# SSM output reloaded into q's slots on SyncE's queue, and rotation tables staged in three tiles with own stores

## The chip, the cores and the metric

The kernel runs on one core of a Trainium2 chip. A core has five engines with their own instruction streams: TensorE (PE, matmuls), VectorE (DVE), ScalarE (ACT), GpSimd (POOL) and SyncE (SP). SP, ACT and POOL also issue DMA transfers, each on its own queue. The metric is the device time of one execution in microseconds (us), given as the median of several runs.

## The reference

One encoder layer over 512 tokens of width 1024, in float32: a half-step SwiGLU FFN, a mixer with two parallel branches (grouped-query attention and a bidirectional S5 state-space model, SSM), a second half-step FFN, and a gated per-layer embedding.

```python
h = h + 0.5 * swiglu(rms_norm(h, ffn1_norm[i]), ffn1_w_gate[i], ffn1_w_up[i], ffn1_w_down[i])
u = rms_norm(h, mix_norm[i])
proj = u @ w_in[i]
q, k, v, x_ssm, g_attn, g_ssm = jnp.split(proj, IN_SPLITS, axis=-1)
...
y_attn = block_gqa_attention(q, k, v).astype(x.dtype) @ w_attn_branch[i]
...
y_s5 = (y_fwd + y_bwd).reshape(b, s, SSM_WIDTH) + ssm_d[i].astype(f32) * x_ssm.astype(f32)
z = jax.nn.gelu(y_s5).astype(x.dtype)
z = z * jax.nn.sigmoid(z @ ssm_glu_w[i] + ssm_glu_b[i])
y_ssm = z @ w_ssm_branch[i]
merged = jax.nn.sigmoid(g_attn) * y_attn + jax.nn.sigmoid(g_ssm) * y_ssm
h = h + merged @ w_out[i]
h = h + 0.5 * swiglu(rms_norm(h, ffn2_norm[i]), ffn2_w_gate[i], ffn2_w_up[i], ffn2_w_down[i])
```

The SSM runs 32 groups of 16 channels with 64 complex states in both directions. The kernel turns it into matmuls over chunks of 8 tokens, for which it builds tables of powers of the complex step (rotation tables) out of the parameters.

## The kernel before

A float32 product is made as three matmuls: each operand is split into a high part (a cast by ACT, line 554, tiles ah, ph, xh, w_h, z) and the rest (a subtraction by DVE, line 555, al, pl, xl, w_l). So a matmul waits for ACT and then for DVE. The order of instructions on each engine is fixed when the kernel is built, by a scheduler that goes by the order of the program, priorities and its own costs. An engine works its own stream strictly in that order; a DMA queue of an issuing engine stands in the same stream, so an issue that has to wait holds what is behind it.

**First FFN (lines 697 to 745).** Tokens lie along the free axis, 512 wide. In each of two halves, eleven tiles f of 128 hidden features are made: gate product pg and up product pu (24 matmuls of 512 columns each), then DVE multiplies each by rb (lines 721 and 723), ACT takes silu (722), DVE multiplies (724), and ah and al are split off. Then come eight down products pd, each over all eleven ah and al.

**SSM parameters (ssm_params).** A generator whose steps are interleaved with the first FFN by `side`. For four sets gh of eight groups, DVE builds the powers T by doubling (lines 285 to 296; the next set begins with the memsets at line 277 and needs ACT's copies out of T to be over). Each set is then laid out as two tables b of 128 partitions by 1280 numbers in a tile tst (tag w3, two buffers): DVE writes a decay part (303 to 305), ACT copies six pieces out of T (307 to 309), and ACT's queue stores the tile of 640 KB to d_tb in device memory (310). POOL's queue in the same time moves other parameter tables (d_at, d_bt, d_a, d_b).

**Mixer.** The input projection w_in is made in pieces: the SSM's input (X), k and v, q, and sixteen gates of 128 features (proj_T, 24 matmuls pi each). DVE prepares trig and gq into tg (lines 860 to 863), and after the last norm sum ss the token scales rs (586 to 592), dg and, by a matmul pb, the row scale rb. The SSM's blocks give Z, which SP stores to zs_d (985). Attention runs by heads: `scores(hd)` makes products sc, exps p and row sums; their reciprocals go through device memory (r_d stored at 968 in pieces of 4 bytes, R loaded at 1018, both on POOL). `values(hd)` transposes p into ppt, splits ph and pl, and multiplies by vhl into po. While a head runs, one filler runs beside it (`fill`): four gates, then the GLU (`z_load`, `half` with w_ssm_glu), then the branch weights. `z_load` (1026) loads hb, the GLU's bias, and zT, four tiles of 256 KB of the SSM's output, into slots x4l to x7l, which hold the normed input for the gates until the last gate is done; then z is split off zT and the GLU's products pg run. Slots q0 to q7 hold qT of the eight heads.

Of the kernel before, what the change touches and what calls it, by code (L numbers as in the profile page):

```python
# [7 lines left out]
F32 = mybir.dt.float32  # L8
# [9 lines left out]
P = 128  # L18
SEQ = 512
G = 32  # L20
NS = 64
CH = 16
L = 8
NC_ = 64
GB = 4
NB = G // GB
TW = 5 * GB * NC_
# [18 lines left out]
def ssm_params(tc, nc, pk_, px, dp, k):  # L46
# [4 lines left out]
    d = {}  # L51
# [12 lines left out]
    pw = es.enter_context(tc.tile_pool(name="pw1", bufs=1, reuse_waits="tile"))  # L64
# [56 lines left out]
    n, q = expm1_parts(ls, s32, "d", -170.0, 170.0)  # L121
# [8 lines left out]
    n, q = expm1_parts(xr, s32, "x", -87.0, 88.0)  # L130
# [23 lines left out]
    f = math.factorial  # L154
# [103 lines left out]
    n, q = expm1_parts(xr, s32, "y", -87.0, 88.0)  # L258
# [16 lines left out]
    for gh in range(0, G, GH):  # L275
        T = pw.tile([P, 2, GH, NC_ + 2], F32, tag="T", name=f"T{gh}")
        V.memset(T[:, :, :, 0], 0.0)
        V.memset(T[:, :, :, NC_ + 1], 0.0)
        V.memset(T[:, 0, :, 1], 1.0)
        V.memset(T[:, 1, :, 1], 0.0)  # L280
        rkl = pw.tile([P, 2, GH], F32, tag="rkl", name=f"rkl{gh}")
        V.tensor_copy(rkl, rk[:, :, gh:gh + GH])
        n = 1
        tb = pw.tile([P, 2, 2, GH * NC_ // 2], F32, tag="tb", name=f"tbx{gh}")
        while n < NC_:
            br = rkl[:, 0].unsqueeze(2).broadcast_to([P, GH, n])
            bi = rkl[:, 1].unsqueeze(2).broadcast_to([P, GH, n])
            cmul2(T[:, 0, :, 1 + n:1 + 2 * n], T[:, 1, :, 1 + n:1 + 2 * n], T[:, :, :, 1:1 + n], br, bi,
                  tb[:, :, :, :GH * n].rearrange("p a r (g n) -> p a r g n", g=GH))
            n *= 2  # L290
            if n < NC_:
                sq = pw.tile([P, 2, GH], F32, tag="sq", bufs=2, name=f"sq{gh}_{n}")
                ta = pw.tile([P, 2, 2, GH], F32, tag="sqt", name=f"sqt{gh}_{n}")
                cmul2(sq[:, 0], sq[:, 1], rkl, rkl[:, 0], rkl[:, 1], ta)
                rkl = sq
            yield 1.0 + n / 20
        for b in range(gh // GB, (gh + GH) // GB):
            st = pw.tile([P, TW], F32, tag="w3", bufs=2, name=f"tst{b}")
            g0 = b * GB - gh
            N = GB * NC_  # L300
            v = lambda i, w=1: st[:, i * N:(i + w) * N].rearrange("p (g c) -> p g c", c=NC_)
            dv = v(4)
            V.tensor_copy(dv, e8[:, b * GB:(b + 1) * GB].unsqueeze(2).broadcast_to([P, GB, NC_]))
            V.memset(dv[:NS, :, 0], 0.0)
            V.memset(dv[NS:, :, NC_ - 1], 0.0)
            for ri in range(2):
                nc.scalar.copy(v(ri), T[:, ri, g0:g0 + GB, 1:NC_ + 1])
                nc.scalar.copy(v(2 + ri)[:NS], T[:NS, ri, g0:g0 + GB, 0:NC_])
                nc.scalar.copy(v(2 + ri)[NS:], T[NS:, ri, g0:g0 + GB, 2:NC_ + 2])
            nc.scalar.dma_start(d["tb"][b], st)  # L310
            yield 0.5
    es.close()
    pw = es.enter_context(tc.tile_pool(name="pw2", bufs=1, reuse_waits="tile"))
# [23 lines left out]
    for b in range(NB):  # L337
        gs = slice(b * GB, (b + 1) * GB)
# [11 lines left out]
        w3 = pw.tile([P, 3, GB, 2, P], BF16, tag="w3", bufs=2, name=f"wo3{b}")  # L350
# [21 lines left out]
    for m in range(G // 8):  # L372
        gs = slice(m * 8, (m + 1) * 8)
# [39 lines left out]
    for b in range(NB):  # L413
        gs = slice(b * GB, (b + 1) * GB)
# [8 lines left out]
        w3 = pw.tile([P, 3, GB, 2, P], BF16, tag="w3", bufs=2, name=f"wv3{b}")  # L423
# [94 lines left out]
def kernel(  # L518
# [6 lines left out]
    nc = tc.nc  # L525
    V, S, T = nc.vector, nc.scalar, nc.tensor
# [26 lines left out]
    def split(hi, lo, src):  # L553
        S.copy(hi, src)  # L554
        V.tensor_sub(lo, src, hi.bitcast(F32))  # L555
# [202 lines left out]
    with tc.tile_pool(name="f1", bufs=1, reuse_waits="tile") as fp, tc.tile_pool(name="pw", bufs=1, reuse_waits="tile") as pw:  # L758
# [18 lines left out]
        st = Stat()  # L777
# [17 lines left out]
    mp = mx.enter_context(tc.tile_pool(name="mp", bufs=1, reuse_waits="tile"))  # L795
    xs_d = dp.tile([SSMW, SEQ], F32, name="xs_d")
    zs_d = dp.tile([SSMW, SEQ], F32, name="zs_d")
    HH = HD // 2

    def slot(pool, tag, bufs, name, dt=F32):  # L800
        return pool.tile([P, SEQ], dt, tag=tag, bufs=bufs, name=uid(name))
# [11 lines left out]
    def run(*gens):  # L813

        gens = list(gens)
        while gens:
            gens = [g for g in gens if next(g, gens) is not gens]
# [13 lines left out]
    def gate(m):  # L831
# [5 lines left out]

        return proj_T(GA0 + m * P, done)

    ts = []  # L840
    ta = [cp.tile([P, SEQ], F32, tag=f"h{m}", name=f"ta{m}") for m in range(KT)]
    qT = [slot(mp, f"q{hd}", 1, "qT", F32R) for hd in range(NH)]
# [9 lines left out]
    with tc.tile_pool(name="qp", bufs=1, reuse_waits="tile") as qp:  # L852
# [39 lines left out]
        for q in range(4):  # L892
            gs = slice(q * G // 4, (q + 1) * G // 4)
# [52 lines left out]
    def scores(hd):  # L946

        g = hd // (NH // 2)
        pr = prs.setdefault(hd, [])
        nb = a0.tile([P, TT], F32, tag="nb", bufs=3, name=uid("nb"))  # L950
        if hd % 2 == 0:
            sums2[hd // 2] = a0.tile([P, 2, TT], F32, tag="s2", bufs=2, name=uid("s2"))
        sm = sums2[hd // 2][:, hd % 2]
        for t in range(TT):
            sc = bank("mm", uid("sc"))
            tk = slice(t * P, (t + 1) * P)
            T.matmul(sc, qT[hd][:, tk], kh[g], start=True, stop=False)
            T.matmul(sc, qT[hd][:, tk], kl[g], start=False, stop=True)  # L958
            V.tensor_reduce(nb[:, t:t + 1], sc, axis=AX.X, op=ALU.max, negate=True)  # L959
            V.tensor_mul(nb[:, t:t + 1], nb[:, t:t + 1], rq[:, t, hd:hd + 1])  # L960
            p_ = slot(pool_p[hd % 2], "pp", 4, "p")
            S.activation(p_, sc, AF.Exp, bias=nb[:, t:t + 1], scale=rq[:, t, hd:hd + 1], accum_out=sm[:, t:t + 1])  # L962
            pr.append(p_)
            yield
        if hd % 2 == 1:
            s2 = sums2[hd // 2]
            V.reciprocal(s2, s2)
            nc.gpsimd.dma_start(r_d[hd // 2].rearrange("h (t p) -> p h t", p=P), s2)
# [19 lines left out]
    at = mx.enter_context(tc.tile_pool(name="at", bufs=1, reuse_waits="tile"))  # L988
# [6 lines left out]
    def values(hd):  # L995
        pr = prs[hd]
        g = hd // (NH // 2)
        po = bank("pv", uid("po"))
        for kt in range(TT):
            pt = bank("pt", uid("ppt"))  # L1000
            for t in range(TT):
                T.transpose(pt[:, t * P:(t + 1) * P], pr[t][:, kt * P:(kt + 1) * P], ident)  # L1002
            ph, pl = ph_("ph", F32R), ph_("pl", F32R)
            split(ph, pl, pt)
            yield
            vv = vhl[:, kt, g].rearrange("p a d -> p (a d)")
            T.matmul(po, vv, ph, start=kt == 0, stop=False)  # L1007
            T.matmul(po, vv, pl, start=False, stop=kt == TT - 1)
        if hd % 2 == 0:
            po_of[hd // 2] = slot(at, "of", 3, "of")  # L1010
        of = po_of[hd // 2]
        ob = at.tile([HD, SEQ], F32, tag="ob", bufs=1, name=uid("ob"))
        S.copy(ob, po[HD:])
        V.tensor_add(of[(hd % 2) * HD:(hd % 2 + 1) * HD], po[:HD], ob)
        if hd % 2 == 1:
            R = at.tile([P, SEQ], F32, tag="R", bufs=1, name=uid("R"))
            for i in range(2):
                nc.gpsimd.dma_start(R[i * HD:(i + 1) * HD], r_d[hd // 2][i].partition_broadcast(HD))
            V.tensor_mul(of, of, R)
            ohl.append(tuple(slot(at, f"o{c}{hd // 2}", 1, "oT", F32R) for c in "hl"))  # L1020
            split(ohl[hd // 2][0], ohl[hd // 2][1], of)


    yhl, zs = [], []

    def z_load():
        xs_ = lambda k, c, name, dt=F32: slot(xp, f"x{k}{c}", 1, name, dt)
        hb = at.tile([P, 4], F32, name="hb")
        nc.gpsimd.dma_start(hb, w["ssm_glu_b"][0].rearrange("(m p) -> p m", p=P))
        V.tensor_scalar_mul(hb, hb, 0.5)  # L1030
        zs.append((hb, xs_))
        for m in range(4):
            zT = xs_(4 + m, "l", "zT")
            nc.gpsimd.dma_start(zT, zs_d[m * P:(m + 1) * P])
            zh, zl = xs_(m, "h", "z", F32R), xs_(m, "l", "z", F32R)
            split(zh, zl, zT)
            zs.append((zT, zh, zl))

    def half(ww, mc, x, done):

# [23 lines left out]
    def fill(i):  # L1064
        ng = 2 * KT - NG1 - NG2
        if i < ng:
            return gate(NG1 + NG2 + i)
        if i < ng + 2:
            if i == ng:
                z_load()  # L1070
            return half(w["ssm_glu_w"][0], i - ng, [z[1:] for z in zs[1:]], glu_done)
        if i < ng + 6:
            return half(w["w_ssm_branch"][0], i - ng - 2, yhl, ssm_done)
        return iter(())
# [15 lines left out]
        split(mg[m][0], mg[m][1], mt)  # L1090

    for hd in range(NH):
        run(values(hd), fill(hd), *([scores(hd + 1)] if hd < NH - 1 else []))
    for i in range(NH, 2 * KT - NG1 - NG2 + 6):
        run(fill(i))
# [2 lines left out]
    st = Stat()  # L1098
# [13 lines left out]
    with tc.tile_pool(name="f2", bufs=1, reuse_waits="tile") as fp:  # L1112
        st = Stat()
# [106 lines left out]
```

## Time and profile before

| | us |
|---|---|
| median of 3 runs | 1187.05 |
| lowest and highest run | 1185.81, 1188.17 |
| the profiled execution | 1185.39 |
| span of that execution, first to last instruction | 1183.6 |
| PE busy in the span | 1143.2 |
| DVE busy | 774.0 |
| ACT busy | 507.5 |
| POOL busy | 58.5 |

The profile tells what happened in one execution. Times of a timeline are us from the span's start. Busy time is the time in which an engine had an instruction at work; an idle time is given in front of the instruction that ended it, with the work whose end released it. A DMA's time runs from its issue to the landing of its last byte. PEclk is the clock that TensorE was granted, 1.0 being 2.4 GHz and 0.5 being 1.2 GHz; over a window it is a mean.

### The profile page before, as it was taken

How to read it: one execution, taken by the hardware profiler on the slowest of the kernel's cores; microseconds unless marked ns; L12 is line 12 of the kernel's file. 1: busy time of each engine (PE TensorE's matmuls, PEld its weight loads, DVE VectorE, ACT ScalarE, POOL GpSimd, SP SyncE). 2: the span in 40 equal slices, each digit the busy share in tenths (PEclk: the TensorE clock that was granted, in tenths of full speed). 3: DMA queues.
4: the chain of work that ended last, by engine and by line, in shares of the span. 5: the costliest groups of instructions: out<-in, count | busy, mean ns of one | idle time of the engine just before them, and what ended most of it. 6: DMA issues, size and time to landing. Idle time of an engine off the chain costs nothing.

```text
span 1183.6 us, 16482 instructions
## 1 busy us (share of the span) xinstructions
PE 1143.2 (97%) x6150; PEld 943.5 (80%) x6150; DVE 774.0 (65%) x1574; ACT 507.5 (43%) x919; POOL 58.5 (5%) x95
## 2 busy tenths in 40 slices
PE   8999989999999999978898999999999999999998
PEld 7888868888788888867676788888888888888886
DVE  4986798887589848989666867554443344444542
ACT  6484455444345437443656634342322223223331
POOL 1314100000000000000010000000000000000100
PEclk9999999999999999999997999999999999999999
DMA  8739865545968995887552245333323433323422
GB/s 190 171 92 313 256 221 178 161 142 107 271 228 268 298 193 157 250 251 224 132 86 62 45 105 164 88 98 91 89 74 99 128 100 96 88 64 98 157 57 54
DMA packets 253440, 175.97 MB, mean 149 GB/s; under 512 B 34896, under 2 KB 235792, under 8 KB 253360
## 3 DMA queue, kind: packets, MB, share of 16 engines
q1 hardware_dynamic: 246352, 153.20, 46.1%
q0 software_dynamic: 5392, 15.36, 5.0%
q10 hardware_dynamic: 1616, 6.36, 1.6%
q8 instruction: 48, 0.79, 0.3%
q14 instruction: 32, 0.26, 0.1%
HBM read 148.89 MB, written 37.58 MB: 158 GB/s over the span
## 4 chain that ended last, share of the span: by engine, by line
PE 74%; DVE 9%; DMA 8%; SPq 3%; issue 3%; ACT 2%; POOL 0%; ACTq 0%; DVEq 0%; POOLq 0%
PE pg L569 7%; PE pg L571 7%; PE pg L570 7%; PE pd L569 7%; PE pd L571 7%; PE pd L570 7%; PE pu L571 5%; PE pu L569 5%; PE pu L570 5%; DMA d_tb<-tst 2%; SPq L411 1%; PE pge L571 1%; PE po L569 1%; PE po L570 1%; PE po L571 1%
## 5 line engine op out<-in xcount | busy, mean ns | idle before, releaser
L723 DVE TENSOR_TENSOR t<-pu,rb 128x512 f32<-128x512 f32 x44 | 30.4, 692 | 86.4 <-PE pu L571 86.3
L721 DVE TENSOR_TENSOR t<-pg,rb 128x512 f32<-128x512 f32 x44 | 30.4, 691 | 54.6 <-PE pg L571 52.3
L554 ACT CAST ah<-t 128x512 fp32r<-128x512 f32 x44 | 27.3, 621 | 36.6 <-DVE t L724 35.9
L742 DVE SCALAR_TENSOR_TENSOR h<-pd,h 128x512 f32<-128x512 f32 x32 | 22.1, 690 | 30.5 <-PE pd L571 30.5
L722 ACT ACTIVATE t<-t 128x512 f32<-128x512 f32 x44 | 27.8, 632 | 28.4 <-DVE t L721 27.3
L555 DVE TENSOR_TENSOR al<-t,ah 128x512 fp32r<-128x512 f32 x44 | 30.3, 689 | 6.7 <-ACT ah L554 6.6
L724 DVE TENSOR_TENSOR t<-t,t 128x512 f32<-128x512 f32 x44 | 30.4, 691 | 2.3
L959 DVE TENSOR_REDUCE nb<-sc 128x1 f32<-128x512 f32 x32 | 21.7, 686 | 9.0 <-PE sc L958 8.9
L555 DVE TENSOR_TENSOR pl<-ppt,ph 128x512 fp32r<-128x512 f32 x32 | 22.0, 687 | 7.6 <-ACT ph L554 7.6
L554 ACT CAST ph<-ppt 128x512 fp32r<-128x512 f32 x32 | 18.8, 588 | 18.5 <-PE ppt L1002 18.4
L962 ACT ACTIVATE p<-sc,nb,rq 128x512 f32<-128x512 f32 x32 | 24.9, 781 | 3.8 <-DVE nb L960 3.5
L1125 POOL DMA_DIRECT2D pin<-in_p_dram x8 | 4.1, 524 | 400.4 <-PE pd L570 395.3
L579 ACT ACTIVATE xh<-h,gains 128x512 fp32r<-128x512 f32 x24 | 17.4, 724 | 14.0 <-DVE h L742 13.5
L1007 PE MATMUL po<-ph,vhl 128*128 128x512 f32 x32 | 14.3, 446 | 7.6 <-ACT ph L554 7.6
L43 PE MATMUL py<-E,wol 128*128 128x64 bf16 x384 | 18.6, 199 | 2.6 <-DVE E L36 2.2
L1002 PE MATMUL ppt<-ident,p 128*128 128x128 f32 x128 | 20.8, 277 | 0.0
L1002 PEld LDWEIGHTS ppt<-ident,p 128*128 128x128 f32 x128 | 16.6, 143 | 4.6 <-issue 0.2
L43 PEld LDWEIGHTS <-wol 128*128 128x128 bf16 x384 | 15.0, 101 | 5.3 <-issue 3.8
L43 PE MATMUL pv<-U,wv 128*128 128x64 bf16 x384 | 13.9, 193 | 5.4 <-DMA wv<-d_wv 5.4
L43 PEld LDWEIGHTS <-wv 128*128 128x128 bf16 x384 | 12.1, 98 | 7.8 <-DMA wv<-d_wv 6.0
L580 DVE SCALAR_TENSOR_TENSOR xl<-h,gains,xh 128x512 fp32r<-128x512 f32 x24 | 18.0, 749 | 0.4
L33 ACT CAST E<-vv 128x256 bf16<-128x256 f32 x16 | 6.5, 404 | 25.6 <-DVE vv L487 25.4
(1974 smaller groups left out, 3909.7 us busy)
## 6 DMA issues: line engine op xcount, KB each, us to landing
w<-in_ffn_w_gate_dram SPq DMA_DIRECT2D x44, 512.0 KB
w<-in_ffn_w_up_dram SPq DMA_DIRECT2D x44, 512.0 KB
w<-in_w_in_dram SPq DMA_DIRECT2D x26, 512.0 KB
w<-in_ffn_w_down_dram SPq DMA_DIRECT2D x32, 384.0 KB
w<-in_ffn_w_down_dram SPq DMA_DIRECT2D x32, 320.0 KB
d_wo<-wo SPq DMA_DIRECT2D x8, 768.0 KB
d_wv<-wv SPq DMA_DIRECT2D x8, 768.0 KB
wv<-d_wv SPq DMA_DIRECT2D x16, 384.0 KB
```

The lines of the kernel that those rows point to most:

```text
L43: nc.tensor.matmul(o, a[i], b[j], start=start and n == 0, stop=stop and n == 5)
L554: S.copy(hi, src)
L555: V.tensor_sub(lo, src, hi.bitcast(F32))
L569: T.matmul(o, ah, bh, start=start, stop=False)
L570: T.matmul(o, ah, bl, start=False, stop=False)
L571: return T.matmul(o, al, bh, start=False, stop=stop)
L721: V.tensor_mul(t1, gu[0], rb)
L722: S.activation(t1, t1, AF.Silu)
L723: V.tensor_mul(t2, gu[1], rb)
L724: V.tensor_mul(t1, t1, t2)
L962: S.activation(p_, sc, AF.Exp, bias=nb[:, t:t + 1], scale=rq[:, t, hd:hd + 1], accum_out=sm[:, t:t + 1])
L1002: T.transpose(pt[:, t * P:(t + 1) * P], pr[t][:, kt * P:(kt + 1) * P], ident)
```

## The change

Three things are edited.

1. The table tile tst is split into three: dv (128x256, written by DVE, stored by POOL's queue), and two tiles st (tst0 and tst1, 128x512 each, written by ACT, stored by ACT's queue). Each has a tag of its own with two buffers.
2. The four zT go into slots q0 to q3 of the heads already done, and are issued on SP's queue by `z_fetch`: one ahead of head 1, two ahead of head 2, one ahead of head 3.
3. hb's tile and its load move from `z_load` to the beginning of the mixer, in the pool mp.

```diff
--- before.py
+++ after.py
@@ -295,19 +295,23 @@
                 rkl = sq
             yield 1.0 + n / 20
         for b in range(gh // GB, (gh + GH) // GB):
-            st = pw.tile([P, TW], F32, tag="w3", bufs=2, name=f"tst{b}")
-            g0 = b * GB - gh
             N = GB * NC_
-            v = lambda i, w=1: st[:, i * N:(i + w) * N].rearrange("p (g c) -> p g c", c=NC_)
-            dv = v(4)
+            dtb = d["tb"][b].rearrange("p (i n) -> p i n", i=5)
+            dv = pw.tile([P, GB, NC_], F32, tag="dv", bufs=2, name=f"dv{b}")
             V.tensor_copy(dv, e8[:, b * GB:(b + 1) * GB].unsqueeze(2).broadcast_to([P, GB, NC_]))
             V.memset(dv[:NS, :, 0], 0.0)
             V.memset(dv[NS:, :, NC_ - 1], 0.0)
-            for ri in range(2):
-                nc.scalar.copy(v(ri), T[:, ri, g0:g0 + GB, 1:NC_ + 1])
-                nc.scalar.copy(v(2 + ri)[:NS], T[:NS, ri, g0:g0 + GB, 0:NC_])
-                nc.scalar.copy(v(2 + ri)[NS:], T[NS:, ri, g0:g0 + GB, 2:NC_ + 2])
-            nc.scalar.dma_start(d["tb"][b], st)
+            nc.gpsimd.dma_start(dtb[:, 4], dv.rearrange("p g c -> p (g c)"))
+            gs = slice(b * GB - gh, (b + 1) * GB - gh)
+            for i in range(2):
+                st = pw.tile([P, 2, GB, NC_], F32, tag=f"st{i}", bufs=2, name=f"tst{b}_{i}")
+                for ri in range(2):
+                    if i == 0:
+                        nc.scalar.copy(st[:, ri], T[:, ri, gs, 1:NC_ + 1])
+                    else:
+                        nc.scalar.copy(st[:NS, ri], T[:NS, ri, gs, 0:NC_])
+                        nc.scalar.copy(st[NS:, ri], T[NS:, ri, gs, 2:NC_ + 2])
+                nc.scalar.dma_start(dtb[:, 2 * i:2 * i + 2], st.rearrange("p r g c -> p r (g c)"))
             yield 0.5
     es.close()
     pw = es.enter_context(tc.tile_pool(name="pw2", bufs=1, reuse_waits="tile"))
@@ -837,6 +841,8 @@
 
         return proj_T(GA0 + m * P, done)
 
+    hb = mp.tile([P, 4], F32, name="hb")
+    nc.gpsimd.dma_start(hb, w["ssm_glu_b"][0].rearrange("(m p) -> p m", p=P))
     ts = []
     ta = [cp.tile([P, SEQ], F32, tag=f"h{m}", name=f"ta{m}") for m in range(KT)]
     qT = [slot(mp, f"q{hd}", 1, "qT", F32R) for hd in range(NH)]
@@ -1021,20 +1027,21 @@
             split(ohl[hd // 2][0], ohl[hd // 2][1], of)
 
 
-    yhl, zs = [], []
+    yhl, zs, zTs = [], [], []
+
+    def z_fetch(m):
+
+        zTs.append(slot(mp, f"q{m}", 1, "zT"))
+        nc.sync.dma_start(zTs[m], zs_d[m * P:(m + 1) * P])
 
     def z_load():
         xs_ = lambda k, c, name, dt=F32: slot(xp, f"x{k}{c}", 1, name, dt)
-        hb = at.tile([P, 4], F32, name="hb")
-        nc.gpsimd.dma_start(hb, w["ssm_glu_b"][0].rearrange("(m p) -> p m", p=P))
         V.tensor_scalar_mul(hb, hb, 0.5)
         zs.append((hb, xs_))
         for m in range(4):
-            zT = xs_(4 + m, "l", "zT")
-            nc.gpsimd.dma_start(zT, zs_d[m * P:(m + 1) * P])
             zh, zl = xs_(m, "h", "z", F32R), xs_(m, "l", "z", F32R)
-            split(zh, zl, zT)
-            zs.append((zT, zh, zl))
+            split(zh, zl, zTs[m])
+            zs.append((zTs[m], zh, zl))
 
     def half(ww, mc, x, done):
 
@@ -1090,6 +1097,8 @@
         split(mg[m][0], mg[m][1], mt)
 
     for hd in range(NH):
+        for m in {1: (0,), 2: (1, 2), 3: (3,)}.get(hd, ()):
+            z_fetch(m)
         run(values(hd), fill(hd), *([scores(hd + 1)] if hd < NH - 1 else []))
     for i in range(NH, 2 * KT - NG1 - NG2 + 6):
         run(fill(i))
```

What the build makes of it, at three places. First ACT at the turn from gate and up to down in FFN1's first half. t_123 and ah_1642 belong to the tenth tile, t_131 to the eleventh; L722 is silu. Before, from the seventh of the twelve copies of the last set on:

```order
L307 COPY tst_1816<-T_1444 128x256
L308 COPY tst_1816<-T_1444 64x256
L309 COPY tst_1816<-T_1444 64x256
L307 COPY tst_1827<-T_1444 128x256
L308 COPY tst_1827<-T_1444 64x256
L309 COPY tst_1827<-T_1444 64x256
L554 CAST ah_1642<-t_123_1636 128x512
L310 DMA d_tb<-tst_1816 128x1280
L554 CAST w_139h<-w_1770 128x768
L310 DMA d_tb<-tst_1827 128x1280
L722 ACTIVATE t_131_1708<-t_131_1708 128x512
```

and with the change (tile ah_1666 is the tenth, ah_1738 the eleventh; L726 is silu):

```order
L558 CAST w_137h<-w_1767 128x640
L558 CAST ah_1666<-t_123_1660 128x512
L310 COPY tst_0_1845<-T_1468 128x256
L312 COPY tst_1_1849<-T_1468 64x256
L313 COPY tst_1_1849<-T_1468 64x256
L558 CAST w_139h<-w_1794 128x768
L310 COPY tst_0_1860<-T_1468 128x256
L312 COPY tst_1_1864<-T_1468 64x256
L310 COPY tst_0_1845<-T_1468 128x256
L312 COPY tst_1_1849<-T_1468 64x256
L313 COPY tst_1_1849<-T_1468 64x256
L310 COPY tst_0_1860<-T_1468 128x256
```

and further on the same engine:

```order
L313 COPY tst_1_1864<-T_1468 64x256
L312 COPY tst_1_1864<-T_1468 64x256
L313 COPY tst_1_1864<-T_1468 64x256
L726 ACTIVATE t_131_1732<-t_131_1732 128x512
L314 DMA d_tb<-tst_0_1845 128x512
L314 DMA d_tb<-tst_1_1849 128x512
L314 DMA d_tb<-tst_0_1860 128x512
L314 DMA d_tb<-tst_1_1864 128x512
L558 CAST w_140h<-w_1818 128x640
L558 CAST ah_1738<-t_131_1732 128x512
L365 COPY bd_1877<-bb 64x8x16 x2
```

The tenth tile's ah now stands ahead of the twelve copies of the last set; the eleventh's silu still stands behind them. Then POOL, before:

```order
L854 DMA trig<-in_consts_dram 128x512
L856 DMA gq<-in_q_norm_dram 128x64
L857 DMA gq<-in_k_norm_dram 128x64
L1029 DMA hb<-in_ssm_glu_b_dram 128x4x1
L968 DMA r_d_5063<-s_386_6626 128x8x1
L1018 DMA R_6977<-r_d_5063 64x512 x2
L1034 DMA zT_7220<-zs_d 128x512
L968 DMA r_d_5064<-s_428_6890 128x8x1
L1034 DMA zT_7226<-zs_d 128x512
L1034 DMA zT_7232<-zs_d 128x512
L1034 DMA zT_7238<-zs_d 128x512
```

and with the change, ahead of the same stores and loads of r_d and R:

```order
L250 DMA d_b<-d_bt 16x32x128 x8
L845 DMA hb<-in_ssm_glu_b_dram 128x4x1
L860 DMA trig<-in_consts_dram 128x512
L862 DMA gq<-in_q_norm_dram 128x64
L863 DMA gq<-in_k_norm_dram 128x64
L974 DMA r_d_5097<-s_386_6660 128x8x1
L1024 DMA R_7013<-r_d_5097 64x512 x2
L974 DMA r_d_5098<-s_429_6926 128x8x1
```

hb has gone from behind gq to ahead of trig, and no zT is left. On SP the four loads stand between weights, behind the eight stores of Z to zs_d:

```order
L568 DMA w_7658<-in_w_ssm_branch_dram 128x4x256
L991 DMA zs_d<-Z 16x32x64 x8
L568 DMA w_7738<-in_w_ssm_branch_dram 128x4x256
L1035 DMA zT_6900<-zs_d 128x512
L1035 DMA zT_7021<-zs_d 128x512
L1035 DMA zT_7023<-zs_d 128x512
L568 DMA w_7772<-in_w_ssm_branch_dram 128x4x256
L1035 DMA zT_7138<-zs_d 128x512
L568 DMA w_7806<-in_w_attn_branch_dram 128x4x256
```

On ACT the casts of z (L558) come in a row, ahead of ob and the next ph:

```order
L840 ACTIVATE ts_5092<-ts_5092 128x512
L968 ACTIVATE p_7102,s_429_6926<-sc_7097,nb_7048,rq 128x512
L558 CAST z_7260<-zT_6900 128x512
L558 CAST z_7264<-zT_7021 128x512
L968 ACTIVATE p_7128,s_429_6926<-sc_7123,nb_7048,rq 128x512
L558 CAST z_7268<-zT_7023 128x512
L558 CAST z_7272<-zT_7138 128x512
L1019 COPY ob_7010<-po_6902 64x512
L558 CAST ph_7063<-ppt_7058 128x512
```

where before each cast of z stood behind or between casts of ph:

```order
L962 ACTIVATE p_7088,s_428_6890<-sc_7083,nb_7008,rq 128x512
L1013 COPY ob_6974<-po_6866 64x512
L554 CAST z_7222<-zT_7220 128x512
L554 CAST ph_7023<-ppt_7018 128x512
L554 CAST w_617h<-w_7626 128x1024
L554 CAST z_7228<-zT_7226 128x512
L554 CAST ph_7047<-ppt_7042 128x512
L554 CAST oT_6981<-of_6860 128x512
L554 CAST z_7234<-zT_7232 128x512
L962 ACTIVATE p_7128,s_483_7122<-sc_7123,nb_7121,rq 128x512
L962 ACTIVATE p_7152,s_483_7122<-sc_7147,nb_7121,rq 128x512
L554 CAST z_7240<-zT_7238 128x512
```

The instructions of POOL that load zT are gone from between r_d and R, and z's casts are no longer mixed with ph's. In the SSM stage the orders agree up to its eighth block; from there gates, exps, weights and blocks come in a slightly other order. On DVE hb's scaling now stands directly ahead of tg, and tg's last three rows between the first steps of rs.

## Rows read from the trace of the kernel before

**Rows 1.** The page: the span, and busy time of each engine.
```profile
span 1183.6 us, 16482 instructions
...
PE 1143.2 (97%) x6150; PEld 943.5 (80%) x6150; DVE 774.0 (65%) x1574; ACT 507.5 (43%) x919; POOL 58.5 (5%) x95
```

**Rows 2.** Busy time by window; (x) counts instructions, last columns clock, DMA share, GB/s.
```profile
60.00:84.00 24.00, 24.00 (x110) 19.94 (x109) 22.96 (x89) 20.48 (x67) 1.50 (x2) 1.00 0.32 94
120.00:140.00 20.00, 20.00 (x90) 16.58 (x89) 14.94 (x61) 9.61 (x19) 5.06 (x8) 1.00 0.98 323
147.50:159.80 12.30, 6.95 (x21) 4.59 (x21) 9.92 (x17) 8.52 (x19) 0.00 (x0) 0.86 0.78 266
617.10:634.50 17.40, 9.26 (x26) 6.10 (x25) 9.51 (x17) 8.11 (x16) 1.05 (x2) 0.61 0.36 82
408.00:420.00 12.00, 12.00 (x59) 10.03 (x58) 7.68 (x26) 3.15 (x3) 0.00 (x0) 1.00 1.07 351
```

**Rows 3.** PE timeline, first stall: start us, us, instruction, [idle before, releaser].
```profile
149.85 0.51 PE L569 MATMUL pd<-ah,w_137h 128*128 128x512 f32 x1 [1.91 <-ACT ah L554]
...
156.46 0.79 PE L569 MATMUL pd<-ah,w_137h 128*128 128x512 f32 x1 [3.21 <-ACT ah L554]
```

**Rows 4.** ACT timeline there: the first of twelve copies, and the cast behind them.
```profile
144.60 0.41 ACT L307 COPY tst<-T 128x256 f32<-128x256 f32 x1 [3.60 <-DVE T L271]
...
149.18 0.62 ACT L554 CAST ah<-t 128x512 fp32r<-128x512 f32 x1
```

**Rows 5.** DVE waits in 84 to 160: us in total, times, longest.
```profile
DVE tst L303 <- DMA d_tb<-tst: 10.4, 3, 6.3
DVE T L277 <- ACT tst L309: 3.9, 3, 1.7
```

**Rows 6.** DVE timeline there: a table copy, and a gate product.
```profile
137.64 0.29 DVE L303 COPY tst<-e 128x256 f32<-128x256 f32 x1 [2.62 <-DMA d_tb<-tst]
...
138.41 0.69 DVE L721 TENSOR_TENSOR t<-pg,rb 128x512 f32<-128x512 f32 x1
```

**Rows 7.** PE timeline, second stall.
```profile
619.02 0.50 PE L1007 MATMUL po<-ph,vhl 128*128 128x512 f32 x1 [1.42 <-ACT ph L554]
...
627.72 0.80 PE L1007 MATMUL po<-ph,vhl 128*128 128x512 f32 x1 [5.74 <-ACT ph L554]
```

**Rows 8.** POOL timeline there: its DMA issues.
```profile
612.98 0.91 POOL L968 DMA_DIRECT2D r_d<-s  x1
...
616.53 0.54 POOL L1034 DMA_DIRECT2D zT<-zs_d  x1 [1.53 <-PE pi L570]
```

**Rows 9.** DMA issues on POOL: count, KB each, median us to landing.
```profile
d_a<-d_at POOLq DMA_DIRECT2D x16, 256.0 KB, 9.9
...
h<-h_d POOLq DMA_DIRECT2D x8, 256.0 KB, 3.3
...
zT<-zs_d POOLq DMA_DIRECT2D x4, 256.0 KB, 12.3
...
trig<-in_consts_dram POOLq DMA_DIRECT2D x1, 256.0 KB, 3.6
r_d<-s POOLq DMA_DIRECT2D x4, 4.0 KB, 11.9
...
gq<-in_k_norm_dram POOLq DMA_DIRECT2D x1, 32.0 KB, 5.1
...
hb<-in_ssm_glu_b_dram POOLq DMA_DIRECT2D x1, 2.0 KB, 2.6
```

**Rows 10.** DVE timeline, end of the first FFN.
```profile
406.60 0.69 DVE L625 TENSOR_TENSOR ss<-ss,sqv 128x512 f32<-128x512 f32 x1
...
407.44 0.42 DVE L860 TENSOR_TENSOR tg<-trig,gq 128x256 f32<-128x256 f32 x1
...
416.24 0.88 DVE L605 TENSOR_SCALAR dg<-ident,rs 128x128 f32<-128x128 f32 x4
```

**Rows 11.** PE timeline there: the row that needs dg.
```profile
421.99 1.02 PE L607 MATMUL pb<-dg,ones 128*128 128x512 f32 x2
```

## The prediction

> **What bounds the kernel now.** I read the page first: of a span of 1183.6 us TensorE (PE) is busy 1143.2 [rows 1], so 40.4 us are idle and everything else is matmuls in a row. A change that removes no matmul can give back that idle time and the time in which matmuls ran slowly, no more. Then the PE timeline, for where the idle time stands, and the windows around each place, for what it really costs. Two places touch the code of this change.
>
> The first is the turn from gate/up to down in the first half of FFN1. PE idles 1.91 us before 149.85 and 3.21 before 156.46, both times for an ah cast by ScalarE (ACT) [rows 3]. The window 147.5 to 159.8 holds 21 matmuls where 120 to 140 holds 90 in 20 us, at 0.222 us each [rows 2]. At that pace 21 matmuls take 4.7 us, so 12.3 us of window hold 7.6 us of **loss A**: 5.35 us idle, and 2.3 us of slow matmuls (the mean granted clock is 0.86, so a part runs at 1.2 GHz, the lower of the two levels, after PE stood idle).
>
> The second is in the attention stage, at the turn from the gates to the GLU. PE waits for ph, 1.42 us before 619.02 and 5.74 before 627.72 [rows 7]. The window 617.1 to 634.5 holds 26 instructions: 8 transposes of 128 columns and 18 matmuls of 512. At 0.23 and about 0.09 us these need 4.9 us, so 12.5 of 17.4 us are **loss B**: 8.1 idle and the rest slow (mean clock 0.61 [rows 2]).
>
> Who is late? In A it is VectorE (DVE), which feeds ACT. It waited 10.4 us, in three waits, at line 303 for the store of a table tile, and 3.9 us at line 277 for ACT's copies out of T [rows 5]. At 137.64 it has just waited 2.62 us more, and so it is still on the tenth tile's gate product at 138.41 [rows 6]. ACT then has twelve copies of 0.41 us from 144.60 ahead of that tile's ah at 149.18 [rows 4]; the order of ACT, above, shows it. In B, zT (the SSM output) lands 12.3 us after its issue [rows 9], the last one is issued at 616.53, behind r_d, on POOL's queue [rows 8], and z's casts stand among ph's on ACT.
>
> **Staging, term A.** dv gets its own 128 KB tile and a store on POOL; the two st tiles are 256 KB each and go out on ACT's queue. DVE's copy at old line 303 no longer waits for a 640 KB store, so the 10.4 us go. It waits for the store of the dv two back, and all eight now stand some way ahead, before 84 us. Line 277 still waits for ACT (3.9 us). The wait for the st tiles' stores goes to ACT, ahead of their copies. What DVE now does earlier, six copies and twelve memsets, is some 2.4 us (0.29 a copy [rows 6], the memsets much less) in a stretch where it is busy 22.96 of 24 us [rows 2]; it delays DVE by as much there, and nothing waits, because PE outlived a far longer lag of DVE between 100 and 140 without a gap (20.00 of 20 busy [rows 2]). POOL's eight stores stand ahead of d_at in its queue; d_a and d_b feed only later work. The byte count is the same.
>
> The last ah was ready at about 156.4 (PE's release [rows 3]). Without the 10.4 us it would be at 146.0, with ACT's twelve copies still ahead of its silu and their store waits up to 148. PE at full pace would come to it at 149: 149.85 less 1.91, and five matmuls. So I take **−7.0** of 7.6; bounds −7.6 and −0 (the wait only moves to ACT). The reason to go near the full end: ACT is busy 9.61 of 20 us in 120 to 140 [rows 2], so it can take a wait of some us where DVE, with 14.94, could not.
>
> **zT, term B.** Four loads leave POOL and go to SyncE's (SP's) queue into q's slots, three of them long before the place. The last one needs q3, free when the scores of head 3 end, about 612: now 4 us earlier than 616.53, and not behind r_d's 4 KB, which takes 11.9 us, against 3.3 for a 256 KB load of h [rows 9]. Landing after 3.3 to 5 us, zT3 is there at 616 to 617. The casts now stand together on ACT ahead of ob and ph, so a late zT3 holds ph. SP's weight loads are queued behind zT3; these have been issued far ahead of their use. With 4.3 us of matmuls after those scores (19 at 0.23), PE waits 0 to 3 us. What is late next is that ph. I take 1.5 us left: **−11.0** of 12.5; bounds −12.5 and −2 (second rival).
>
> On the queue the trace shows [rows 9]: on POOL a 256 KB load took 3.3 us where little was in flight and 12.3 behind r_d. The Trainium skill ("DMA: Bandwidth & Descriptors", Issuing engines are not separate DMA queues) says that transfers started by different engines share the same sixteen DMA engines, and that spreading them saves only the time to issue. By that, SP's queue would not shorten the landing and B would be about −2; rows 9 cannot tell whether the queue or the engines held zT, and a rival below prices it.
>
> **hb, term C.** Hidden in the diff: hb's load now stands on POOL ahead of trig and both gq (order of POOL, above), and its tile takes memory which DVE's last ss add reads until 407.3 [rows 10]. Before, trig and gq had landed before 407.44, where tg starts. Now the four DMAs are issued from 407.3 on, 0.6 to 0.9 each (like rows 8), the last at about 409.5. On DVE, hb's scaling and tg stand ahead of w_311l and of the rsqrt chain whose dg starts at 416.24 and takes 0.88 [rows 10]; PE needs dg for pb at 421.99 [rows 11]. That is 4.9 us of cover, and some 2 more from DVE's own gaps (7.68 of 12 us busy [rows 2]): tg may start up to 414.4. With gq's 5.1 us the last landing is 414.5: **cost 0**. With the 9.9 us of d_a (DMA share 0.98 then, 1.07 here [rows 2, 9]) it is 419.4: **cost 5**. hb itself goes in 4-byte pieces: 2.6 us in a quiet stretch, r_d with twice the pieces 11.9. Between the ends I take **+2.5**, nearer d_a because of the 1.07. No gain can come of it.
>
> **Order in the SSM stage, term D.** The new tiles change some places of gates, exps and weight loads between 525 and 590. No work is added. Outside A and B 26.9 us of idle are left in the kernel (40.4 less 5.35 and 8.1); I take 0 with 3 us to both sides, about a tenth of that. hb's earlier load frees nothing at 575, where nothing waited.
>
> **Sum.** The profiled execution took 1185.39 us, against a median of 1187.05, so 1.7 less. 1185.4 − 7.0 − 11.0 + 2.5 + 0 = 1169.9 for an execution like it; from the median, 1187.05 − 15.5, **1171.5 us**. What follows is worked from the median.
>
> **Rivals.**
> 1. Staging only moves the wait. The stores of two tiles back hold ACT's copies instead, silu and ah stand behind these, and weights' casts too. For it: stores lasted so long that DVE waited 6.3 us once [rows 5], with DMA at 0.98. Against: ACT's slack, and dv out of the chain. A is 0: 1187.05 − 11 + 2.5 = 1178.6. Chance 0.12.
> 2. zT3 lands after 12.3 us on SP too: at 624, and z's last cast, ob and ph some 1.7 us later, so PE goes on at 625.7 instead of 627.72 and as slowly as before. B is −2: 1187.05 − 7 − 2 + 2.5 = 1180.6. For it: r_d's pieces are in flight at the same time whatever the queue. Against: the h loads' 3.3 on a queue with nothing in small pieces ahead. Chance 0.12.
> 3. **Slower.** C's chain, hb's pieces first and trig and gq behind, at a DMA share above 1: 11.9 for hb, 9.9 for trig after it, and 5.1 for gq are 27 from 408, so 435; tg is 20.6 us beyond its 414.4, and the sum is 1187.05 − 18 + 20.6, 1189.7. It decides from a landing at 432 on. Against: these transfers overlap, and the longest median of this size in the trace is 12.3. Chance 0.07.
> 4. It does not do what it says: SP holds zT until late, behind the weight ahead of the last load, and A keeps half: within 0.2% only if C costs 5 or more besides. Chance 0.04.
>
> **How the numbers follow.** The forecast has the remaining 0.65. The low end: A −7.6, B −12.5, C 0, D −3 give 1164.0. The high end: rival 1 with C at its 5 gives 1181.1, rival 2 gives 1180.6, and 1 us more for D: 1182. Less than 2 in 10 is outside: rivals 3 and 4 above (0.11) and little below. A measurement of this kernel tells some 0.2% (2.4 us) from no change. Faster: forecast and rivals 1 and 2, 0.89; same 0.04; slower 0.07.
>
> **What would show it.** A: no DVE wait at the dv copy, PE idle below 1 us between 145 and 160, clock 1.0. If wrong: ACT waiting for d_tb stores ahead of the tst copies. B: zT landing in 3 to 5 us, PE idle below 3 us between 612 and 630. If wrong: ACT waiting at z for zT. C: hb and trig issued after 407, DVE waiting at hb or tg, PE waiting for dg at about 420; over 7 us there would break the forecast. D: PE's idle time between 525 and 590 as before within 3 us.

## The result

The changed kernel takes 1174.2 us (median of 4 runs, 1171.3 to 1177.3), against 1186.43 for the kernel before beside it (1185.47 to 1188.17): a ratio of 0.9896, 95% interval 0.9863 to 0.9929. Two further comparisons gave 0.9879 (0.9858 to 0.9900) and 0.9876 (0.9853 to 0.9899). It is faster by 12 to 15 us; 1171.5 was predicted, with 1164 to 1182 as the range.

The page of the changed kernel, the two lines that answer to [rows 1]:

```profile
span 1174.4 us, 16499 instructions
...
PE 1142.6 (97%) x6150; PEld 943.1 (80%) x6150; DVE 772.5 (66%) x1574; ACT 506.1 (43%) x917; POOL 60.6 (5%) x99
```

The span is 9.2 us shorter in this execution, one of the slower of its four, and PE's busy time is the same: what has gone is idle time, 40.4 us before and 31.8 now.

The same two places by windows, as in [rows 2] (PE busy and its count, then PE's weight loads and the other engines, clock, DMA share, GB/s):

```profile
147.50:159.80 12.30, 9.96 (x37) 7.74 (x36) 10.49 (x18) 7.90 (x17) 0.00 (x0) 0.86 0.75 248
610.00:630.00 20.00, 19.37 (x97) 15.73 (x96) 18.09 (x35) 16.45 (x34) 1.97 (x3) 1.00 0.29 77
617.10:634.50 17.40, 16.77 (x88) 13.49 (x87) 15.89 (x31) 13.76 (x27) 1.04 (x2) 1.00 0.17 47
```

At the turn of the first FFN PE now does 37 matmuls in 12.3 us where it did 21, but 55 would fit (0.222 us each), so a part of loss A is still there. At the turn from the gates to the GLU, 610 to 630, PE is busy 19.37 of 20 us at full clock, and in the window of [rows 2] 16.77 of 17.4 us where it was 9.26: loss B is gone.

To see where the difference arises, I read five marks in every trace: the second copy of pb into rb (end of the first FFN), the first Gelu of the SSM's output (line 978 before, 984 now), PE's row of a gate product pi that waits 1.7 us for p of the first head (586.38 before, 587.59 now; the SSM stage ends there and the attention stage begins), the first silu of the second FFN, and the end of the span. Differences of the marks, in us:

| trace | to rb | rb to first Gelu | SSM stage | attention | second FFN on |
|---|---|---|---|---|---|
| before | 423.1 | 52.8 | 110.5 | 193.5 | 403.7 |
| changed | 419.3 | 53.4 | 114.9 | 182.8 | 404.0 |
| changed, second trace (again) | 417.2 | 52.8 | 112.3 | 183.7 | 404.1 |
| changed, third trace (again2) | 420.9 | 52.8 | 114.2 | 183.9 | 404.0 |

So the first FFN gives 2.2 to 5.9 us, the attention stage 9.6 to 10.7, and the SSM stage takes 1.8 to 4.4 back in these three.

Term A's place. PE's row with the largest wait there, and ACT's rows ahead of it, from the timelines of the changed kernel (start us, us, instruction, [idle before, releaser]):

```profile
151.28 0.50 PE L573 MATMUL pd<-ah,w_137h 128*128 128x512 f32 x1 [2.33 <-ACT ah L558]
```

```profile
142.52 0.41 ACT L310 COPY tst<-T 128x256 f32<-128x256 f32 x1 [1.52 <-DVE T L271]
...
147.44 0.40 ACT L313 COPY tst<-T 64x256 f32<-64x256 f32 x1
147.87 0.63 ACT L726 ACTIVATE t<-t 128x512 f32<-128x512 f32 x1
...
150.61 0.62 ACT L558 CAST ah<-t 128x512 fp32r<-128x512 f32 x1 [1.49 <-DVE t L728]
```

The first of the last set's twelve copies starts at 142.52 when DVE has finished T, the last at 147.44; only then comes the eleventh tile's silu, 147.87, and its ah at 150.61. PE came to it at 148.95 (151.28 less 2.33). The tenth tile's ah, on which PE waited before [rows 3, 4], is cast at 140.38, long ahead.

What DVE and ACT wait for between 56 (84 for ACT) and 160 us (us in total, times, longest), to be read beside [rows 5]:

```profile
DVE T L277 <- ACT tst L313: 8.4, 3, 4.1
DVE w_140l L559 <- ACT w_140h L558: 3.1, 1, 3.1
DVE w_121l L559 <- ACT w_121h L558: 3.0, 1, 3.0
DVE w_136l L559 <- ACT w_136h L558: 1.8, 1, 1.8
```

```profile
ACT w_121h L558 <- DMA w<-in_ffn_w_up_dram: 3.8, 1, 3.8
ACT w_137h L558 <- DMA w<-in_ffn_w_down_dram: 3.0, 1, 3.0
...
ACT tst L312 <- DMA d_tb<-tst: 1.1, 1, 1.1
```

The 10.4 us of DVE at the table copy are gone, and no dv copy waits. ACT waits 1.1 us for a table's store: the wait has not simply moved. But DVE's wait for ACT's copies out of T has grown from 3.9 to 8.4 us, and casts of weights are waited for: ACT waits 3.8 us for one up weight and 3.0 for the second down weight. In this trace these weights land no later than before; ACT comes to them earlier. The up weight's cast, before and with the change:

```profile
115.44 1.03 ACT L554 CAST w_121h<-w 128x1024 fp32r<-128x1024 f32 x1
```

```profile
115.23 1.05 ACT L558 CAST w_121h<-w 128x1024 fp32r<-128x1024 f32 x1 [3.76 <-DMA w<-in_ffn_w_up_dram]
```

So most of the 10.4 us came back as other waits ahead of T (4.5 us more at line 277, 3.0 and 1.8 at two weights), and T is finished only 2.1 us earlier than before: ACT's first copy out of it starts at 142.52, against 144.60 in [rows 4].

Term B's place. SP's issues and POOL's r_d, then ACT's casts:

```profile
596.79 3.09 SPq L1035 DMA_DIRECT2D zT<-zs_d  x3
...
610.33 0.32 SPq L1035 DMA_DIRECT2D zT<-zs_d  x1
```

```profile
615.09 0.93 POOL L974 DMA_DIRECT2D r_d<-s  x1 [12.94 <-DVE s L973]
```

```profile
612.64 1.15 ACT L558 CAST z<-zT 128x512 fp32r<-128x512 f32 x2
...
614.43 1.16 ACT L558 CAST z<-zT 128x512 fp32r<-128x512 f32 x2
...
616.22 0.59 ACT L558 CAST ph<-ppt 128x512 fp32r<-128x512 f32 x1
```

The last zT is issued at 610.33, 6.2 us earlier than [rows 8], and 4.8 us ahead of r_d; its cast, the second of the row at 614.43, waits for nothing.

Term C's place, POOL and DVE at the end of the first FFN, beside [rows 9, 10]:

```profile
397.57 0.78 POOL L845 DMA_DIRECT2D hb<-in_ssm_glu_b_dram  x1 [264.70 <-DVE ss L629]
398.34 0.56 POOL L860 DMA_DIRECT2D trig<-in_consts_dram  x1
```

```profile
402.87 0.68 DVE L629 TENSOR_TENSOR ss<-ss,sqv 128x512 f32<-128x512 f32 x1
...
403.70 0.17 DVE L1039 TENSOR_SCALAR hb<-hb 128x4 f32<-128x4 f32 x1
403.78 0.42 DVE L866 TENSOR_TENSOR tg<-trig,gq 128x256 f32<-128x256 f32 x1
...
412.45 0.87 DVE L609 TENSOR_SCALAR dg<-ident,rs 128x128 f32<-128x128 f32 x4
```

hb was issued at 397.57, five us ahead of the last ss add (402.87) and not behind it. hb landed after 3.5 us, trig after 4.9, gq after 4.2 and 4.5; tg at 403.78 waits for nothing, 0.2 us after the last of these landings (399.43 + 4.2).

### The profile page after: what moved, and what is told of

Read it like the earlier page. It is cut to its first block, busy times and chain, and to the rows that moved or that the text cites. A ratio compares the mean times of both kernels' runs of the same rounds, so it can differ in the third digit from the quotient of the medians.

```text
span 1174.4 us, 16499 instructions
## 1 busy us (share of the span) xinstructions
PE 1142.6 (97%) x6150; PEld 943.1 (80%) x6150; DVE 772.5 (66%) x1574; ACT 506.1 (43%) x917; POOL 60.6 (5%) x99
## 4 chain that ended last, share of the span: by engine, by line
PE 71%; DVE 12%; DMA 9%; SPq 3%; ACT 3%; issue 2%; ACTq 0%; DVEq 0%
PE pd L573 7%; PE pd L575 7%; PE pd L574 7%; PE pg L575 6%; PE pg L573 6%; PE pg L574 6%; PE pu L575 5%; PE pu L573 5%; PE pu L574 5%; DMA w<-in_ffn_w_down_dram 2%; PE pi L573 2%; PE pi L574 2%; PE pi L575 2%; SPq L415 1%; DMA d_tb<-tst 1%
## 5 line engine op out<-in xcount | busy, mean ns | idle before, releaser
L558 ACT CAST ah<-t 128x512 fp32r<-128x512 f32 x44 | 27.4, 622 | 43.2 <-DVE t L728 42.4
L726 ACT ACTIVATE t<-t 128x512 f32<-128x512 f32 x44 | 27.8, 632 | 14.7 <-DVE t L725 13.6
L558 ACT CAST ph<-ppt 128x512 fp32r<-128x512 f32 x32 | 18.8, 587 | 16.8 <-PE ppt L1008 16.7
L583 ACT ACTIVATE xh<-h,gains 128x512 fp32r<-128x512 f32 x24 | 17.4, 723 | 13.9 <-DVE h L746 13.4
L43 PE MATMUL py<-U,ml 128*128 128x64 bf16 x192 | 10.8, 196 | 6.8 <-DMA ml<-d_m 6.8
L1174 DVE SCALAR_TENSOR_TENSOR sg<-sg,ple 128x512 f32<-128x512 f32 x8 | 5.4, 686 | 16.7 <-PE ple L575 16.7
```

Of the source, the lines that this page charges most:

```text
L43: nc.tensor.matmul(o, a[i], b[j], start=start and n == 0, stop=stop and n == 5)
L726: S.activation(t1, t1, AF.Silu)
```

## The experiments

Each kernel was run beside the kernel before on the same chip; ratios are to that. First the parts apart and the changed kernel again.

**The changed kernel again (again, again2).** No edit.

> The changed kernel once more, beside the three below. Its four runs lay between 1171.3 and 1177.3 us, at mean granted clocks of 0.990 to 0.996. Theory: the spread is the SSM stage, where TensorE waits for DMAs and its clock falls in some executions and not in others; then this trace has another number of slow stretches between 500 and 590 us, and the same waits (about 2.3 us) at the turn of the first FFN. Rival: the spread comes from the first FFN's turn or from the attention stage, and the SSM stage is as in the first trace (100.9 us from the wait for ml at 486.6 to the gate product at 587.6, where before it was 96.5).

> The changed kernel, as the partner of the next run on the same chip, since the earlier pair differed by 2.3 us with spreads of 4 to 6. Expected as before, 1172 to 1176 us.

1174.38 us (ratio 0.9879) and 1174.75 (0.9876). The theory held in part: by the marks above the SSM stage took 114.9, 112.3 and 114.2 us in the three traces. Of the 2.6 us between the first and the second, half is idle time of PE (16.1 and 14.9 us) and half slower matmuls (98.8 and 97.5 us busy; the mean clock of the stage was 0.94 and 0.95). This window of the two shows a place where the clock differs:

```profile
500.00:510.00 10.00, 7.98 (x78) 6.63 (x74) 6.61 (x16) 2.54 (x6) 0.00 (x0) 0.83 0.94 265
```

```profile
500.00:510.00 10.00, 10.00 (x125) 8.54 (x122) 8.18 (x19) 2.85 (x6) 0.00 (x0) 1.00 0.88 246
```

In the first trace PE had waited 2.02 us for ml at 502.70 and part of the window ran at 1.2 GHz; in the second it had waited 1.22, up to 499.81, and the window is at 2.4 GHz throughout. The theory failed in its second half: the wait at the first turn varies too, 2.33, 2.15 and 4.48 us in the three; in the third ACT waits 6.6 us for the second down weight, where it waited 3.0 in the first. In these three traces the spread, some 6 us, comes from both places.

**Staging alone (staging_only).** The kernel before with the edit of lines 297 to 310 and nothing else.

> The kernel before with the three staging tiles alone. The instruction order from 160 us on is that of before. Theory: what the trace of the change showed at the first stall, 3.6 us less up to the wait for w_233 at 315 us, and the rest unchanged: 1182.8 us. Rival 1: the SSM stage, which waits for DMAs, gives part of it back: 1184 to 1186. Rival 2, the prediction's own size of 7 us: 1179.4.

1183.05 us, ratio 0.9954 (0.9938 to 0.9971): 5.5 us less, between the theory's 3.6 and the rival's 7. Its first FFN ends at 418.9 on the mark rb, its SSM stage is 111.5 us, one more than before's.

**zT and hb alone (zt_only).** The changed kernel with before's table staging.

> The kernel before with zT in q's slots on SP's queue and hb at the mixer's start, table staging as before. Theory: the second stall goes (10 to 12 us less from the gate product at 586 on), and the new order in the SSM stage costs 1 to 4 us there: 1176 to 1180 us. Rival: the new order costs nothing, and the longer SSM stage of the first trace of the change was its clock by chance: 1174 to 1176, with the stage from the wait for ml to the first gate after it at 96.5 us, give or take 1.

1178.66 us, ratio 0.9916 (0.9897 to 0.9935): 10 us less, inside the theory's range. The attention stage takes 182.8 us, as in the changed kernel, the SSM stage 112.5, two us more than before's. The parts add up: 5.5 and 10.0 make 15.5, against 12.3 to 14.7 for both together, with intervals of 2 us on each.

**The last copies behind ah (late_copies, late_copies2).** The changed kernel, with the copies of the last set made to follow the eleventh tile's ah on ACT; the generator is held for one step and gets it back.

```diff
+        if gh + GH == G:
+            yield 6
...
+                with k["behind"](gh + GH == G):
...
-            yield 0.5
+            yield 0.5 - 6 * (b == NB - 1)
...
+    kd["behind"] = lambda on: tc.issue_after(last_ah[0].ins) if on else ExitStack()
```

> The changed kernel with the twelve table copies of the last set behind the eleventh tile's ah on ScalarE (the kernel's generator is held back for one step). Theory: what was left of the first stall (2.3 us idle and the slow matmuls behind it) is those copies standing ahead of silu and ah; it goes, 3 to 4 us less than the changed kernel beside it. Rival: the down weights land too late by then (TensorE's next wait names a cast of w behind a DMA), and nothing or under 1 us is gained.

> The changed kernel with the last twelve table copies behind the eleventh ah, once more beside the changed kernel. Theory: the 2 us idle at the first turn and the slow matmuls behind it are gone in every execution: 2 to 4 us under its partner. Rival: what was gained there is lost again in the SSM stage, which waits for DMAs: within 1 us of its partner.

1172.07 us (0.9864, 0.9840 to 0.9887) and 1171.05 (0.9856, 0.9831 to 0.9880), 2.3 and 3.7 us under the changed kernel beside it by the medians; the intervals overlap, but the traces are plain. The lines are of the first. PE by window, and ACT:

```profile
147.00:160.00 13.00, 13.00 (x59) 10.76 (x58) 7.65 (x13) 9.72 (x23) 0.00 (x0) 1.00 0.67 216
```

```profile
148.00 0.62 ACT L736 CAST ah<-t 128x512 fp32r<-128x512 f32 x1 [1.81 <-DVE t L733]
148.53 0.71 ACT L313 COPY tst<-T 128x256 f32<-128x256 f32 x2
```

The eleventh ah is at 148.00 with the copies behind it, PE is busy for all 13 us, and no PE row between 20 and 300 us waits (in the second trace one waits, 0.2 us for a weight in the gate and up products; the turn has none). The late weights, which the rival named, were there (ACT waits 3.12 us for the third down weight at 144.20) and cost PE nothing. By its medians this version is the fastest of all that were run; its intervals overlap with those of the changed kernel and of zt_pool.

**The copies behind ah, with the old staging (late_only).** The same edit on the kernel before.

> The kernel before, its old staging tiles kept, with the last set's twelve copies behind the eleventh tile's ah. Theory: both causes count; VectorE still waits 10 us for the stores and is still at the tenth tile's gate product at about 138, so the eleventh's ah comes at 149 to 152 and 2 to 4 us of the first stall's 7.6 stay: 3 to 5 us less than before. Rival 1: the order of ScalarE alone was the cause, the stall goes: 6 to 8 us less. Rival 2: VectorE's lag alone was: under 2 us less.

1185.11 us, ratio 0.9977 (0.9959 to 0.9995), 2.7 us less, between the theory's 3 to 5 and the second rival's 2. DVE's wait and PE's:

```profile
DVE tst L305 <- DMA d_tb<-tst: 11.8, 3, 6.5
```

```profile
153.55 0.50 PE L572 MATMUL pd<-ah,w_137h 128*128 128x512 f32 x1 [2.85 <-ACT ah L732]
```

DVE still waits 11.8 us for the stores, the eleventh ah comes at 152.88, and PE still idles 2.85 us there, and 0.83 us for a weight at 147.52. So neither edit alone removes loss A, and both together do.

**zT on SP's queue, old slots (zt_spq).** One word on the kernel before. In the build the casts of z move up some places on ACT with it, past a weight's cast, one ph and two exps.

```diff
-            nc.gpsimd.dma_start(zT, zs_d[m * P:(m + 1) * P])
+            nc.sync.dma_start(zT, zs_d[m * P:(m + 1) * P])
```

> The kernel before with one word changed: zT is loaded by SP's queue instead of POOL's, into the same slots x4l to x7l and at the same place. Theory: the queue held it. The slots are free as before (the last at 616.5), the landing takes 3 to 5 us instead of 12.3 since r_d's small pieces are no longer ahead, PE's long wait at ph shrinks from 5.7 to under 2 us: 5 to 8 us less than before. Rival: the engines held it, whatever the queue: landings of 10 to 13 us, the wait stays, no change within 2 us.

1187.47 us, ratio 0.9989 (0.9973 to 1.0005): no change. The theory fell. The issues, the first cast and PE's first long wait:

```profile
611.33 4.45 SPq L1034 DMA_DIRECT2D zT<-zs_d  x4
```

```profile
611.87 0.93 POOL L968 DMA_DIRECT2D r_d<-s  x1 [8.88 <-DVE s L967]
```

```profile
620.43 0.62 ACT L554 CAST z<-zT 128x512 fp32r<-128x512 f32 x1 [6.15 <-DMA zT<-zs_d]
```

```profile
621.71 0.79 PE L1007 MATMUL po<-ph,vhl 128*128 128x512 f32 x1 [4.91 <-ACT ph L554]
```

The first zT is issued on SP's queue at 611.33, half a us ahead of r_d on POOL's, and is there only at 620.43, nine us later. The next two casts of z wait for their loads too, until 623.61 and 625.76, so it is the landings that are late and not only the order on ACT. Another queue did not help. A weight of 512 KB, issued at 610.09, stands ahead of the four on SP, so what held them was still open between r_d, the weight and the rest.

**zT on POOL's queue, new slots (zt_pool).** The reverse, on the changed kernel: `nc.sync` to `nc.gpsimd` in z_fetch.

> The changed kernel with zT on POOL's queue, still into q's slots. Theory: the slots matter as much as the queue: the last zT is issued at about 610 and stands ahead of r_d there, lands in 3 to 5 us, and the time is that of the changed kernel within 2 us. Rival: POOL's queue is the trouble itself (zT behind the first r_d and R): landings of 10 us or more, PE waits 3 to 6 us at ph or z, 4 to 8 us more than the changed kernel.

1172.99 us, ratio 0.9875 (0.9844 to 0.9906): the same as the changed kernel. The landings, and POOL's issues:

```profile
DMA to landing us min/median/max: 3.4/3.5/5.0
```

```profile
605.16 0.54 POOL L1035 DMA_DIRECT2D zT<-zs_d  x1 [2.99 <-PE sc L964]
609.66 0.91 POOL L974 DMA_DIRECT2D r_d<-s  x1 [3.95 <-DVE s L973]
```

On POOL's queue zT lands in 3.4 to 5.0 us. The last is issued at 605.16, and r_d only 4.5 us later.

**r_d in rows (rd_rows).** The kernel before with r_d of heads 2 and 3 stored as 128 rows of 32 bytes. The same 4 KB are written, in another order than R's loads go by, so the scales of these two heads are left out of place. All engines' orders are as before.

```diff
-            nc.gpsimd.dma_start(r_d[hd // 2].rearrange("h (t p) -> p h t", p=P), s2)
+            if hd == 3:
+                nc.gpsimd.dma_start(r_d[1].rearrange("h s -> (h s)").rearrange("(p x) -> p x", p=P), s2.rearrange("p h t -> p (h t)"))
```

> The kernel before, with every order as it was; only the store of the row sums' reciprocals of heads 2 and 3 (r_d, 4 KB) goes out as 128 rows of 32 bytes in place of 1024 pieces of 4 bytes, so these two heads are scaled by wrongly ordered sums. Theory, after zT landed as late on SP's queue as on POOL's: r_d's pieces hold the DMA engines themselves while they are in flight, whatever queue zT stands on. Then r_d lands in 2 to 4 us, zT in 3 to 5 instead of 12.3, PE's waits at ph of 1.4 and 5.7 us come down to 2 together, and the time is 6 to 9 us under before. Rival: the weights in flight or the end of the gates hold zT; landings stay at 9 to 12 us and the time within 2 us of before.

1177.74 us, ratio 0.9925 (0.9896 to 0.9953), 9 us less; the landings of zT, in the kernel before and here, and the window that answers to loss B:

```profile
DMA to landing us min/median/max: 5.3/12.3/13.3
```

```profile
DMA to landing us min/median/max: 2.9/3.3/3.3
```

```profile
616.00:634.50 18.50, 17.49 (x89) 13.60 (x88) 17.57 (x33) 16.08 (x32) 1.88 (x4) 1.00 0.29 92
```

zT, on POOL's queue in x's old slots, three of the four behind this r_d, and with the same weights in flight, lands in 2.9 to 3.3 us, and PE is busy 17.49 of 18.5 us. r_d itself lands in 2.9 us, where it took 12.0. That settles it for POOL's queue: 4 KB in 1024 pieces of 4 bytes held the loads behind it for some nine us. The kernel before shows it by order too: its first zT, issued at 612.39, 0.6 us ahead of r_d, landed in 5.3 us, and the three behind r_d took 11.9 to 13.3. That the same pieces held zT on SP's queue in zt_spq fits, but no run has SP's queue with r_d in rows, so the weight's part there is not separated.

## Why the prediction was right, and where it was not

The sum said 15.5 us less; 12 to 15 were measured, and 13.2 come out of the marks below. The sign, the two places and their order of size were right. That the total came so near is in part luck: A and B gave 2.8 us less than forecast and D took about 2 that were not in the sum, while C's 2.5 did not come, so the errors cancel in part. Term by term:

**A, predicted −7.0, measured −5.1.** By the mark rb, four traces with the old staging (before 423.1, zt_only 424.8, zt_spq 422.5, rd_rows 425.9) have a median of 424.0, five with the new (419.3, 417.2, 420.9, 418.9 and zt_pool 418.7) one of 418.9. By time, staging_only says 5.5. The step that was mis-sized is "without the 10.4 us it would be at 146.0, ... up to 148". It let the whole of DVE's wait for stores vanish, and kept the wait for ACT at 3.9 us. In the changed kernel the latter is 8.4 us, and DVE and ACT wait besides for weights to which they now come before these land, so T is finished 2.1 us earlier and not 10.4. The copies out of it stand ahead of silu and bring ah to 150.6, about 1.7 us after PE comes to it, and its cast has to run yet. The prediction's sign for A (PE idle below 1 us between 145 and 160, clock 1.0) failed with 2.3 us and 0.89. late_copies shows that this order is what was left: with it gone PE does not wait at all and rb comes at 415.9 and 414.8. The first rival (the wait moves to ACT's copies) took place to 1.1 us only.

**B, predicted −11.0, measured −10.1.** The attention stage has a median of 193.0 us in four traces with old slots and old r_d (193.5, staging_only 192.2, zt_spq 192.6, late_only 193.8) and of 182.9 in the three of the changed kernel, zt_only and zt_pool (182.8, 183.7, 183.9, 182.8, 182.9; the two of late_copies have 181.2 and 183.8); rd_rows, with old slots, has 181.2. The size was near. The step that failed is the reason: "not behind r_d's 4 KB" in POOL's queue. zt_spq and zt_pool show that the queue does not matter beyond the noise, and rd_rows that r_d's pieces do. So the culprit was named rightly and the cure wrongly; that the number came out all the same is luck in so far as the slots alone, which the prediction credited with an issue 4 us earlier, brought all of it (zt_pool). What the change does is to issue the last zT while r_d of heads 2 and 3 has not begun: the q slots come free before the head's sums are complete, x's slots only with the last gate. The second rival was right that another queue does not shorten the landing, and its size was wrong, because it let r_d be in flight together with the last zT: r_d was issued 4.8 us later than that. The Trainium skill ("DMA: Bandwidth & Descriptors", Issuing engines are not separate DMA queues) says that transfers run on the same sixteen DMA engines whichever engine started them, and that issuing from several saves only the time to issue; the ratio of 0.9989 in zt_spq agrees.

**C, predicted +2.5, measured 0.** "Its tile takes memory which DVE's last ss add reads" was misread: the trace of the changed kernel has hb issued at 397.57, behind the add before the last one, so hb, trig and gq go out at about the time at which trig did before, and land in 3.5 to 4.9 us. dg follows the last ss add by 9.6 us, as before (412.45 and 402.87, against 416.24 and 406.60 in [rows 10]). zt_only shows the same again: hb goes out at 405.18, behind the add before the last one, the landings are 3.3 to 4.9 us, tg starts at 411.38, 0.9 us after the last ss add (410.47), and PE does not wait for dg either. The third rival, which needed a landing at 432, was far off: the last came at 403.6.

**D, predicted 0 within 3, measured about +2.** With the old order of the SSM stage five traces take 110.5, 111.5, 110.2, 114.3 and 110.5 us (before, staging_only, zt_spq, late_only, rd_rows), with the new one seven (the three of the changed kernel, zt_only, zt_pool, and the two of late_copies) take 114.9, 112.3, 114.2, 112.5, 110.6, 111.0 and 112.5. The medians, 110.5 and 112.5, differ by 2 us, but both orders have traces near 110 and above 114: that the new order costs something is possible and not shown. The first trace of the changed kernel alone would have said 4.4.

What the prediction did not foresee is the spread: it called some 0.2% (2.4 us) what a measurement of this kernel can tell, and runs of the changed kernel beside each other spread over 4 to 7 us, those of the kernel before over up to 10 (1181.9 to 1192.1 beside rd_rows).

## What to carry to other kernels

When a wait is removed from one engine, look at what stands ahead of the waited-for instruction on the next engine too: rb comes 5.1 us earlier with the new tables and 8.6 with the copies behind ah as well, so the order on ACT had kept 3.5 us back. Here a late landing that coincided with a store in 4-byte pieces was not cured by another queue; issuing the load before the store, or storing in longer rows, did cure it. And one trace per kernel is not enough where a stage waits for DMAs: compare marks over several traces before putting a few us down to an edit.

## What the runs showed of the hardware

r_d's 1024 pieces of 4 bytes took 9 to 12 us from issue to landing. 256 KB loads issued behind them on POOL's queue took 11.9 to 13.3 us in the kernel before, and the first on SP's queue in zt_spq about nine; the one issued just ahead of them on POOL's took 5.3, and those of zt_pool and rd_rows 2.9 to 5.0. In the kernel before, the pieces of heads 2 and 3 cost 9 us (rd_rows). How they hold the loads is not shown: while three zT were outstanding there, the DMA engines' share of busy time, the last column but one, was low:

```profile
618.00:621.00 3.00, 1.16 (x3) 0.67 (x4) 2.62 (x6) 1.88 (x3) 0.00 (x0) 0.89 0.12 34
621.00:624.00 3.00, 0.98 (x5) 0.58 (x3) 1.68 (x2) 0.00 (x0) 0.00 (x0) 0.50 0.22 27
```

The changed kernel's SSM stage took 112 to 115 us from one execution to the next. In its window from 500 to 510 us the mean granted clock was 0.83 in the two traces in which PE had waited 2.02 and 1.91 us for ml, a part at 1.2 GHz, and 1.00 in the one in which it had waited 1.22.
